# GLA mixer: states and outputs of two chunks at a time, their float32 products in one row

## The chip, the core and the metric

One Trainium2 chip, one of its cores. The core has five engines that run their own instruction lists and wait for each other by semaphores: PE (matmuls into PSUM), DVE and ACT (elementwise work, both can read PSUM), POOL (elementwise work outside PSUM) and SP (here it only issues DMAs). In a profile, PEld is PE's weight load, which overlaps its matmuls. The metric is device microseconds of one execution, the median of the runs.

## What is computed

Two layers on x of shape (1, 1024, 1024): a gated linear attention (GLA) layer with four heads, then a Mamba-2 layer. The change lies in the GLA layer. Of its reference, per head, with q, k, a of 128 columns and v of 512:

```python
def step(S, inp):
    qi, ki, vi, ai = inp
    b = jnp.cumsum(ai, axis=-2)
    o_inter = jnp.einsum('bhcd,bhdv->bhcv', qi * jnp.exp(b), S)
    ...
    o = o_inter + jnp.einsum('bhij,bhjv->bhiv', attn, vi)
    b_last = b[:, :, -1:, :]
    S = jnp.exp(b_last[:, :, 0, :, None]) * S + jnp.einsum(
        'bhjd,bhjv->bhdv', ki * jnp.exp(b_last - b), vi)
    return S, o
...
o = rmsnorm(o, w_head_norm).reshape(bsz, L, GLA_DV) * jax.nn.silu(g.astype(jnp.float32))
return o.astype(h.dtype) @ w_out
```

## The kernel before

The sequence is cut into two halves of 512 tokens (t = 0 and 1) and each half into four chunks of 128 tokens (the result does not depend on the chunk's size). The program is GLA on half 0, GLA on half 1, then the Mamba-2 layer on both. Large projections are "units" of 12 matmuls with 512 columns each: both operands are split into a float32r high and low part, and three products are summed (`mm3`, L223 to L225; L469 to L471 for v). Their PSUM tiles are called pp, the weight tiles wh and wl: ACT casts the high part (L171), POOL subtracts to get the low part (L176), four units ahead of PE.

The mixer of a head is a generator (`mixer`) that advances beside the units: after each unit, some of its steps are emitted, and a scheduler then sets the order on each engine, PE's too, from what it thinks is ready. The mixer's PSUM tiles are called mb; there are four of them in turn. For the part that changes:

- `split(c)` makes the high and low part of v of chunk c (ACT L649, POOL L650).
- `state(c, parts)` is three float32r matmuls of 512 columns into one mb tile: the chunk's addition to the state S (PE L223 to L225 with mb<-t,ktok). A step of DVE then makes the next S (L717 for the first, L719), in one of four tiles x.
- The outputs of a chunk are, for each of four blocks of 128 columns, a float32 matmul of S with qd (L712, left out where there is no S yet) and one of v with at (L713), into an mb tile po. The trace shows a float32 matmul as two records.
- po is then copied to SBUF: two blocks by ACT (L726), two by DVE (L727), into o0 and o1 (o2 in the code).
- After four chunks: squares and their sum on ACT and POOL, silu gate times output on POOL (L737), the norm's sum over partitions on PE (L292, L293), a chain on DVE and ACT (L299, L311 to L313, L745) and the high and low parts yh and yl (ACT L748, DVE L749), which the units of the output projection take (pp<-yh,wh).

In the last half, no state is made after the last chunk (nst is 3).

Of the kernel before, what the change touches and what calls it, by code (L numbers as in the profile page):

```python
# [14 lines left out]
ALU = mybir.AluOpType  # L15

P = 128
T = 512
# [3 lines left out]
NC = T // P  # L22
# [3 lines left out]
ORDER = mybir.DependencyInfo(mybir.DependencyClass.NoSync, mybir.DependencyReason.DATA)  # L26
# [27 lines left out]
def hybrid_kernel(ctx: ExitStack, tc: tile.TileContext, xT, w_in0, w_gk, w_up, w_out0,  # L54
                  w_in1, w_dt, w_out1, par, masks, tri, out):
    nc = tc.nc
    V, A, G, PE = nc.vector, nc.scalar, nc.gpsimd, nc.tensor
    dma = nc.sync.dma_start
# [12 lines left out]
    def tl(tag, bufs, shape=(P, T), dt=F32):  # L71
        cnt[0] += 1
        return sb.tile(list(shape), dt, name=f"{tag}_{cnt[0]}", tag=tag, bufs=bufs)

    def ps(tag):
        cnt[0] += 1
        return (psp if tag == "pp" else psm).tile([P, T], F32, name=f"{tag}_{cnt[0]}", tag=tag)

    def tmp(n=P):
        t = tl("t", NTMP)  # L80
        return t[:] if n == P else t[0:n, :]

    def c3(ap, w=P):
        return ap.rearrange("p (n w) -> p n w", w=w)
# [5 lines left out]
    def act(out, in_, func, **k):  # L90
        name = SILU if func == AF.Silu else LN_EXP
        i = None
        if name != table[0]:
            i = A.preload_act_table_set(name)
            for m in table[2]:
                tc.add_manual_dep(i.ins, m.ins.name, ORDER, reason="table")
            table[:] = name, i, []
        o = A.activation(out, in_, func, **k)
        tc.add_manual_dep(o.ins, table[1].ins.name, ORDER, reason="table")
        table[2].append(o)  # L100
        return o


    pr = cst.tile([P, N_PAR], F32, name="pr")
# [17 lines left out]
    at = cst.tile([P, NC, P], F32, name="at")  # L122

    def late_constants():
        mskf = tmp()
        dma(mskf[:, 0:N_MASK], masks)
        dma(trim[:], tri)
        G.memset(a64[:], 0.0)
        G.memset(at[:], 0.0)
        V.tensor_copy(msk[:], mskf[:, 0:N_MASK])  # L130
        V.tensor_tensor(idd[:], ident[0:64, 0:32], ident[0:64, 32:64], op=ALU.add)
        act(ea_log[:], pr[0:32, C_AL:C_AL + 1], AF.Exp)
# [5 lines left out]
    S_carry = [dram.tile([P, T], F32, name=f"S_{h}") for h in range(GH)]  # L138
# [83 lines left out]
    def mm3(o, lh, ll, rh, rl, first, last):  # L222
        PE.matmul(o, lh, rh, start=first, stop=False)  # L223
        PE.matmul(o, lh, rl, start=False, stop=False)  # L224
        PE.matmul(o, ll, rh, start=False, stop=last)  # L225
# [71 lines left out]
    def rstd_of(p, n, box, var, stay=False):  # L297
        v = tmp() if var is None else var
        V.tensor_scalar(v, p[:], 1.0 / n, EPS, op0=ALU.mult, op1=ALU.add)  # L299
        r = p[:] if stay else tl("rstd", 3)[:]  # L300
        l = tmp()
        act(l, v, AF.Ln)
        act(l, l, AF.Exp, scale=-0.5)
        newton(V, r, v, l)
        box.append(r)
        yield
# [102 lines left out]
    class Gla:  # L409
# [115 lines left out]
        def mixer(self, h):  # L525
# [7 lines left out]
            V.tensor_tensor(wup[64:96, :], wraw[64:96, :], wup[64:96, :].bitcast(F32), op=ALU.subtract)  # L533
            S = None
            if t:
                S = tl("x", 4)[:]
                dma(S, S_carry[h][:])
            yield
# [4 lines left out]
            m, l = tmp(), tmp()  # L543
# [5 lines left out]
            for c in range(NC):  # L549
                cs = slice(c * P, (c + 1) * P)  # L550
# [9 lines left out]
            dec = tl("decg", 2, (P, NC))  # L560
# [6 lines left out]
            qd = tl("x", 4)[:]  # L567
# [61 lines left out]
            for c in range(NC):  # L629
                cs = slice(c * P, (c + 1) * P)  # L630
                PE.transpose(ptk[:, cs], kd[:, cs], ident[:])

            o2 = [tl(tag, 1, (P, 2, T))[:] for tag in ("o0", "o1")]
# [9 lines left out]
            v = self.v[h]  # L643
            nst = NC - 1 if t == NT - 1 else NC

            def split(c):
                if c < nst:
                    vh, vl = tl("t", NTMP, dt=F32R)[:], tl("t", NTMP, dt=F32R)[:]
                    A.copy(vh, v[c])  # L649
                    G.tensor_tensor(vl, v[c], vh.bitcast(F32), op=ALU.subtract)  # L650
                    return vh, vl
# [5 lines left out]
            last = []  # L657

            def half_columns(o, lhsT, rhs):
                m = PE.matmul(o, lhsT, rhs, start=True, stop=True)  # L660
                if last:
                    tc.add_manual_dep(m.ins, last[-1].ins.name, ORDER, reason="columns")
                last.append(m)

            def products(p, kk, qq, w, c0, c1):
                for c in range(c0, c1):
                    for hh in range(2):
                        ks, qs, o = c * P + hh * 64, (2 * (c - c0) + hh) * w, (c - c0) * w
                        half_columns(p[hh * 64:hh * 64 + 64, o:o + w], kk[:, ks:ks + 64], qq[:, qs:qs + w])
                return p[:, 0:(c1 - c0) * w]  # L670
# [5 lines left out]
            for c in range(NC):  # L676
                half_columns(p64[c], d[:, c * P:c * P + 64], d[:, c * P + 64:(c + 1) * P])
# [11 lines left out]
            vp = split(0)  # L689
# [3 lines left out]
            o = [o2[vb // 2][:, vb % 2, :] for vb in range(4)]  # L693
            def state(c, parts):
                if c < nst:
                    p = ps("mb")
                    cs = slice(c * P, (c + 1) * P)
                    mm3(p[:], kh[:, cs], kl[:, cs], *parts, True, True)
                    return p

            pst = state(0, vp)
            vp = split(1)
            for g in self.g[h]:
                act(g, g, AF.Silu)
            yield
            for c in range(NC):
                cs = slice(c * P, (c + 1) * P)
                po = ps("mb")
                for vb in range(4):
                    vs = slice(vb * P, (vb + 1) * P)  # L710
                    if S is not None:
                        PE.matmul(po[:, vs], S[:, vs], qd[:, cs], start=True, stop=False)  # L712
                    PE.matmul(po[:, vs], v[c][:, vs], at[:, c, :], start=(S is None), stop=True)  # L713
                if c < nst:
                    Sn = tl("x", 4)[:]
                    if S is None:
                        V.tensor_copy(Sn, pst[:])  # L717
                    else:
                        V.scalar_tensor_tensor(Sn, S, dec[:, c:c + 1], pst[:], op0=ALU.mult, op1=ALU.add)  # L719
                    S = Sn  # L720
                    if c == NC - 1:
                        dma(S_carry[h][:], S)
                pst = state(c + 1, vp)
                vp = split(c + 2)
                yield
                A.copy(o2[0][:, :, cs], c3(po[:, 0:256]))  # L726
                V.tensor_copy(o2[1][:, :, cs], c3(po[:, 256:T]))  # L727
            yield


# [12 lines left out]
            for vb in range(4):  # L743
# [3 lines left out]
                c = tl("yl", 6, dt=F32R)[:]  # L747
# [486 lines left out]
    def mixq(g, h, rate):  # L1234
        return [[Lazy(lambda: g.mixer(h)), rate, 0.0]]
# [6 lines left out]
    for p in range(2):  # L1242
        g = ph[p]
        for h in range(GH):
            o = [lambda: g.outp(h - 1)] if h else ([lambda: ph[0].outp(3)] if p else [])
# [16 lines left out]
    for p in range(2, 4):  # L1262
        s = ph[p]
        for g in range(SG):
# [18 lines left out]
            elif p == 3 and g == SG - 2:  # L1283
# [3 lines left out]
                last = mixq(s, g + 1, 1.0)[0]  # L1287
# [120 lines left out]
```

## Time and profile before

| | |
|---|---|
| median of 3 runs | 1597.12 us (1595.63 to 1600.03) |
| profiled execution, its own time | 1597.23 us |
| its span from first to last instruction | 1595.5 us |
| mean granted TensorE clock | 0.997 of full speed |
| busy share PE / PEld | 98% / 82% |
| busy share DVE / ACT / POOL | 58% / 60% / 41% |

A busy share is averaged over the whole span. PE's is made of matmuls whose ends are modelled, so what a matmul costs is better read from start to start. The GLA mixers lie between about 56 and 760 us.

### The profile page before, as it was taken

What the parts mean: (1) busy time and instruction counts of PE and PEld (TensorE: products, weight loads), DVE (VectorE), ACT (ScalarE), POOL (GpSimd) and SP (SyncE); (2) the same over time, 40 slices, a digit from 0 to 9 for tenths busy, and PEclk for the clock granted to TensorE, in tenths of its full rate; (3) what the DMA queues carried; (4) which work ended last, traced back from release to release, by engine and by line L of the source; (5) the groups of instructions that cost most, each with busy time, mean ns of one, the idle gap of its engine ahead of it and who ended that gap; (6) DMA issues with size and microseconds to landing.
All of it is one profiled execution on the core that took longest, in us unless ns stands there. A gap on an engine that the chain in (4) does not pass through costs nothing.

```text
span 1595.5 us, 24009 instructions
## 1 busy us (share of the span) xinstructions
PE 1566.5 (98%) x8272; PEld 1304.9 (82%) x8272; DVE 919.1 (58%) x1579; ACT 955.2 (60%) x1804; POOL 651.2 (41%) x542
## 2 busy tenths in 40 slices
PE   7999999999999999999999999999999999999996
PEld 5787888888888888888888888888878888888886
DVE  7355557595516245396735445447967963355657
ACT  4455455564627355474866757666667677767843
POOL 6455565643320111227345665666513222222322
PEclk9999999999999999999999999999999999999999
DMA  7544566565675465554685565666765776655752
GB/s 237 190 152 145 167 193 198 174 208 161 206 249 178 155 202 185 172 187 141 198 283 163 185 210 189 187 201 198 246 197 197 242 230 217 201 182 187 264 190 86
DMA packets 172746, 309.30 MB, mean 194 GB/s; under 512 B 19088, under 2 KB 25104, under 8 KB 172624
## 3 DMA queue, kind: packets, MB, share of 16 engines
q1 hardware_dynamic: 172624, 307.77, 60.3%
q8 instruction: 65, 1.06, 0.3%
q14 instruction: 57, 0.47, 0.1%
HBM read 232.06 MB, written 75.63 MB: 193 GB/s over the span
## 4 chain that ended last, share of the span: by engine, by line
PE 84%; DVE 5%; ACT 5%; DMA 4%; issue 1%; POOL 1%; SPq 0%; DVEq 0%; POOLq 0%; ACTq 0%
PE pp L223 20%; PE pp L224 20%; PE pp L225 20%; PE pp L469 4%; PE pp L471 4%; PE pp L470 4%; PE mb L713 2%; PE mb L712 2%; PE mb L959 2%; PE mb L660 2%; DMA wraw<-w_in 1%; PE mb L952 1%; DMA v<-a_cum 1%; PE mb L223 1%; PE mb L224 1%
## 5 line engine op out<-in xcount | busy, mean ns | idle before, releaser
L171 ACT CAST wh<-wraw 128x512 fp32r<-128x512 f32 x472 | 289.8, 618 | 354.1 <-PE pp L224 136.9
L223 PE MATMUL pp<-hh,wh 128*128 128x512 f32 x1184 | 467.9, 396 | 8.7 <-ACT wh L171 7.6
L224 PE MATMUL pp<-hl,wh 128*128 128x512 f32 x1184 | 464.1, 392 | 1.2 <-DVE hl L371 1.2
L225 PE MATMUL pp<-hh,wl 128*128 128x512 f32 x1184 | 462.8, 391 | 0.0
L176 POOL TENSOR_TENSOR wl<-wraw,wh 128x512 fp32r<-128x512 f32 x240 | 322.5, 1352 | 313.2 <-ACT wh L171 245.0
L223 PEld LDWEIGHTS pp<-hh,wh 128*128 128x128 f32 x1184 | 222.7, 188 | 59.5 <-ACT wh L171 9.0
L224 PEld LDWEIGHTS pp<-hl,wh 128*128 128x128 f32 x1184 | 223.0, 188 | 48.6 <-DVE hl L371 3.1
L225 PEld LDWEIGHTS pp<-hh,wl 128*128 128x128 f32 x1184 | 222.9, 188 | 46.1
L223 PE MATMUL pp<-yh,wh 128*128 128x512 f32 x448 | 177.0, 397 | 2.6 <-DVE acc L515 1.2
L225 PE MATMUL pp<-yh,wl 128*128 128x512 f32 x448 | 176.0, 393 | 0.0
L224 PE MATMUL pp<-yl,wh 128*128 128x512 f32 x448 | 175.6, 392 | 0.0
L469 PE MATMUL pp<-wh,hh 128*128 128x512 f32 x256 | 99.9, 393 | 2.7 <-DVE m L444 2.7
L223 PEld LDWEIGHTS pp<-yh,wh 128*128 128x128 f32 x448 | 84.2, 188 | 22.3 <-ACT acc L889 2.4
L650 POOL TENSOR_TENSOR t<-v,t 128x512 fp32r<-128x512 f32 x28 | 39.3, 1414 | 153.4 <-ACT t L649 98.2
L470 PE MATMUL pp<-wl,hh 128*128 128x512 f32 x256 | 100.4, 392 | 0.0
L471 PE MATMUL pp<-wh,hl 128*128 128x512 f32 x256 | 100.0, 393 | 0.0
L225 PEld LDWEIGHTS pp<-yh,wl 128*128 128x128 f32 x448 | 84.1, 188 | 18.8
L224 PEld LDWEIGHTS pp<-yl,wh 128*128 128x128 f32 x448 | 84.2, 188 | 18.2 <-DVE yl L749 0.3
L830 DVE SCALAR_TENSOR_TENSOR m<-pp,pr,m 128x509 f32<-128x509 f32 (+2 forms) x96 | 70.5, 744 | 43.4 <-ACT m L827 42.4
L321 POOL TENSOR_TENSOR ss<-ss,t 128x512 f32<-128x512 f32 x53 | 75.1, 1417 | 42.5 <-ACT t L320 32.3
L830 DVE SCALAR_TENSOR_TENSOR x<-pp,pr,x 128x509 f32<-128x509 f32 (+2 forms) x96 | 71.2, 744 | 32.1 <-ACT x L827 30.9
L1041 POOL TENSOR_TENSOR t<-t,o 128x512 fp32r<-128x512 f32 x32 | 42.2, 1322 | 94.0 <-ACT o L1039 93.9
(287 smaller groups left out, 2593.9 us busy)
## 6 DMA issues: line engine op xcount, KB each, us to landing
wraw<-w_in SPq DMA_DIRECT2D x352, 256.0 KB, 3.6
low_in<-wl SPq DMA_DIRECT2D x176, 256.0 KB, 3.9
wl<-low_in SPq DMA_DIRECT2D x176, 256.0 KB, 3.1
wraw<-w_out SPq DMA_DIRECT2D x128, 256.0 KB, 3.4
low_out<-wl SPq DMA_DIRECT2D x64, 256.0 KB, 3.8
v<-a_cum SPq DMA_DIRECT2D x64, 256.0 KB, 3.8
wl<-low_out SPq DMA_DIRECT2D x56, 256.0 KB, 3.1
xn<-x SPq DMA_DIRECT2D x43, 256.0 KB, 3.7
```

Of the source, the lines that this page charges most:

```text
L171: A.copy(hi[:, 0:w], raws[n][:, 0:w])
L176: G.tensor_tensor(lo[:, 0:w], raws[n][:, 0:w], hi[:, 0:w].bitcast(F32), op=ALU.subtract)
L223: PE.matmul(o, lh, rh, start=first, stop=False)
L224: PE.matmul(o, lh, rl, start=False, stop=False)
L225: PE.matmul(o, ll, rh, start=False, stop=last)
L321: eng.tensor_tensor(ss, ss, sq, op=ALU.add)
L469: PE.matmul(o, rh[kb][:, cs], wh[:], start=(kb == 0), stop=False)
L470: PE.matmul(o, rh[kb][:, cs], wl[:], start=False, stop=False)
L471: PE.matmul(o, rl[kb][:, cs], wh[:], start=False, stop=(kb == KB - 1))
L650: G.tensor_tensor(vl, v[c], vh.bitcast(F32), op=ALU.subtract)
L830: V.scalar_tensor_tensor(dst[:, s:], o[:, 0:T - s], col(C_CW + j * 32 + si), dst[:, s:], op0=ALU.mult, op1=ALU.add)
L1041: G.tensor_tensor(xel[-1], xe, hi.bitcast(F32), op=ALU.subtract)
```

## The change

The four passes of a loop over chunks become two pairs. The states of chunks 0 and 1 come first, then the outputs of both chunks, chunk 1 ahead of chunk 0; then the states of 2 and 3, then their outputs. Within a pair, each float32 matmul is made to follow the one before it in PE's order (`behind`, which only orders; other matmuls may still be put between). The pair's two PSUM tiles are taken at once and copied out together. No instruction is added and none removed; the number of yields in this part, six, stays.

```diff
+    def behind(m, last):
+        if last:
+            tc.add_manual_dep(m.ins, last[-1].ins.name, ORDER, reason="columns")
+        last.append(m)
...
+            def outputs(c, Ss):
+                last, po = [], [ps("mb") for _ in range(2)]
+                for i in (1, 0):
+                    cs = slice((c + i) * P, (c + i + 1) * P)
+                    for vb in range(4):
+                        vs = slice(vb * P, (vb + 1) * P)
+                        if Ss[i] is not None:
+                            behind(PE.matmul(po[i][:, vs], Ss[i][:, vs], qd[:, cs], start=True, stop=False), last)
+                        behind(PE.matmul(po[i][:, vs], v[c + i][:, vs], at[:, c + i, :], start=(Ss[i] is None),
+                                         stop=True), last)
+                return po
...
-            for c in range(NC):
-                cs = slice(c * P, (c + 1) * P)
-                po = ps("mb")
-                for vb in range(4):
-                    vs = slice(vb * P, (vb + 1) * P)
-                    if S is not None:
-                        PE.matmul(po[:, vs], S[:, vs], qd[:, cs], start=True, stop=False)
-                    PE.matmul(po[:, vs], v[c][:, vs], at[:, c, :], start=(S is None), stop=True)
-                if c < nst:
-                    Sn = tl("x", 4)[:]
...
-                pst = state(c + 1, vp)
-                vp = split(c + 2)
-                yield
-                A.copy(o2[0][:, :, cs], c3(po[:, 0:256]))
-                V.tensor_copy(o2[1][:, :, cs], c3(po[:, 256:T]))
-            yield
+            S1 = step(S, 0, pst)
+            pst = state(1, vp)
+            vp = split(2)
+            yield
+            po = outputs(0, (S, S1))
+            S = step(S1, 1, pst)
+            pst, vp = state(2, vp), split(3)
+            yield
+            evac(0, po)
+            S3 = step(S, 2, pst)
+            pst = state(3, vp)
+            yield
+            po = outputs(2, (S, S3))
+            S = step(S3, 3, pst)
+            if S is not None:
+                dma(S_carry[h][:], S)
+            yield
+            evac(2, po)
+            yield
```

`evac(c, po)` is the two copies (now L731 and L732) for both chunks of the pair, and `step` the DVE instruction that makes the next S (now L710 and L712). Lines of the changed kernel lie 6 higher in `mm3` and before the mixer, up to 29 higher behind it.

The order that the scheduler makes of it differs at these places. PE, first head of half 0, from the last projection matmul ahead of the first outputs (mb_190 holds the outputs of chunk 0, mb_192 the state of chunk 1, mb_203 the outputs of chunk 1); before:

```order
L469 MATMUL pp_199_988<-wh_216_1077,hh5_34_197 128x512
L713 MATMUL mb_190_964<-at_86,v_113_566 128x128 x4
L223 MATMUL mb_192_971<-t_188_955,ktok_157_758 128x512
L224 MATMUL mb_192_971<-t_189_956,ktok_157_758 128x512
L225 MATMUL mb_192_971<-t_188_955,t_158_759 128x512
L712 MATMUL mb_203_1007<-x_146_708,x_191_969 128x128
L713 MATMUL mb_203_1007<-at_86,v_114_568 128x128
```

The same place in the changed kernel (mb_203 holds the outputs of chunk 1, mb_202 those of chunk 0, mb_205 and mb_212 the states of chunks 2 and 3):

```order
L476 MATMUL pp_198_983<-wl_209_1025,hh4_27_180 128x512
L723 MATMUL mb_203_1001<-x_146_708,x_190_964 128x128
L477 MATMUL pp_198_983<-wh_208_1024,hl4_28_181 128x512
...
L476 MATMUL pp_200_985<-wl_209_1025,hh4_27_180 128x512
L724 MATMUL mb_203_1001<-at_86,v_114_568 128x128
...
L724 MATMUL mb_202_1000<-at_86,v_113_566 128x128 x4
L229 MATMUL mb_205_1016<-t_192_970,ktok_157_758 128x512
...
L229 MATMUL mb_212_1050<-t_206_1020,ktok_157_758 128x512
```

The state of chunk 1 has moved ahead of all outputs. The first float32 matmul stands alone, six projection matmuls ahead of the rest of its pair; then the other eleven follow each other, and then two states in a row.

DVE, the same head, from the second S on (x is S; o1 is the copy of a po); before:

```order
L727 COPY o1_150_723<-mb_190_964 128x2x128
L719 SCALAR_TENSOR_TENSOR x_204_1016<-x_191_969,decg_141_682,mb_192_971 128x512
L727 COPY o1_150_723<-mb_203_1007 128x2x128
L719 SCALAR_TENSOR_TENSOR x_212_1057<-x_204_1016,decg_141_682,mb_205_1018 128x512
L727 COPY o1_150_723<-mb_211_1048 128x2x128
```

and in the changed kernel:

```order
L712 SCALAR_TENSOR_TENSOR x_204_1014<-x_190_964,decg_141_682,mb_191_966 128x512
L732 COPY o1_150_723<-mb_203_1001 128x2x128
L732 COPY o1_150_723<-mb_202_1000 128x2x128
L712 SCALAR_TENSOR_TENSOR x_211_1048<-x_204_1014,decg_141_682,mb_205_1016 128x512
L712 SCALAR_TENSOR_TENSOR x_215_1072<-x_211_1048,decg_141_682,mb_212_1050 128x512
L732 COPY o1_150_723<-mb_214_1055 128x2x128
L732 COPY o1_150_723<-mb_213_1054 128x2x128
```

The third S (x_211), which the second pair of outputs needs, now stands behind the two copies of the first pair.

ACT, third head of half 0, behind the table load that follows the gates' silu (t is the high part of a chunk of v, v_433 that of chunk 1); before:

```order
L94 ACT_TABLE_LOAD
L171 CAST wh_528_2594<-wraw_512_2484 128x512
L320 ACTIVATE t_534_2625<-xn_508_2473 128x512
L171 CAST wh_535_2628<-wraw_520_2538 128x512
L649 CAST t_540_2654<-v_433_2151 128x512
L171 CAST wh_542_2663<-wraw_526_2573 128x512
```

and in the changed kernel:

```order
L94 ACT_TABLE_LOAD
L177 CAST wh_535_2628<-wraw_520_2538 128x512
L177 CAST wh_542_2663<-wraw_526_2573 128x512
L326 ACTIVATE t_534_2625<-xn_508_2473 128x512
L177 CAST wh_551_2698<-wraw_530_2600 128x512
L655 CAST t_540_2654<-v_433_2151 128x512
```

The split of chunk 1 now stands behind the cast of a weight three units further on (wh_551, wh_552 before).

## Rows read from the trace of the kernel before

**Rows 1.** The page, part 1: busy us, share of the span, instructions.

```profile
PE 1566.5 (98%) x8272; PEld 1304.9 (82%) x8272; DVE 919.1 (58%) x1579; ACT 955.2 (60%) x1804; POOL 651.2 (41%) x542
```

**Rows 2.** Busy time by stage: stretch, length, then busy of each engine.

```profile
core 0: us, PE busy (x) PEld busy (x) DVE busy (x) ACT busy (x) POOL busy (x), PEclk, DMA share, GB/s
60.00:400.00 340.00, 338.46 (x1779) 281.88 (x1778) 207.11 (x403) 183.10 (x328) 182.30 (x142) 1.00 0.56 175
400.00:760.00 360.00, 360.00 (x1892) 300.81 (x1891) 188.59 (x386) 188.77 (x346) 93.39 (x74) 1.00 0.58 186
```

**Rows 3.** PE's waits between 60 and 760 us, all there are.

```profile
PE pp L223 <- DVE acc L515: 1.2, 1, 1.2
PE pp L223 <- ACT yh L748: 0.3, 1, 0.3
```

**Rows 4.** Timeline of PE, first head of half 0: start, length, instruction.

```profile
99.82 0.39 PE L469 MATMUL pp<-wh,hh 128*128 128x512 f32 x1
...
105.94 0.39 PE L469 MATMUL pp<-wh,hh 128*128 128x512 f32 x1
106.17 1.05 PE L713 MATMUL mb<-at,v 128*128 128x128 f32 x8
...
107.53 0.39 PE L225 MATMUL mb<-t,t 128*128 128x512 f32 x1
107.77 0.38 PE L712 MATMUL mb<-x,x 128*128 128x128 f32 x2
...
109.32 0.39 PE L713 MATMUL mb<-at,v 128*128 128x128 f32 x2
109.47 0.48 PE L223 MATMUL mb<-t,ktok 128*128 128x512 f32 x1
...
110.25 0.40 PE L470 MATMUL pp<-wl,hh 128*128 128x512 f32 x1
```

**Rows 5.** Timeline of PE at the end of that head's mixer.

```profile
136.14 0.39 PE L293 MATMUL mb<-t,onr 128*128 128x512 f32 x1
...
143.86 0.39 PE L225 MATMUL pp<-hh,wl 128*128 128x512 f32 x1
144.58 0.47 PE L223 MATMUL pp<-yh,wh 128*128 128x512 f32 x1 [0.34 <-ACT yh L748]
145.09 0.50 PE L224 MATMUL pp<-yl,wh 128*128 128x512 f32 x1
```

**Rows 6.** Timelines of ACT, POOL and DVE at that end.

```profile
117.00 0.37 ACT L726 COPY o<-mb 128x256 f32<-128x256 f32 x1 [2.12 <-PE mb L713]
...
117.45 5.09 POOL L737 TENSOR_TENSOR sg<-o,sg 128x512 f32<-128x512 f32 x4 [3.17 <-ACT o L726]
...
131.76 1.36 DVE L290 TENSOR_TENSOR t<-ss,t 128x512 fp32r<-128x512 f32 x1 [13.93 <-ACT t L289]
136.57 0.69 DVE L299 TENSOR_SCALAR t<-mb 128x512 f32<-128x512 f32 x1 [3.44 <-PE mb L293]
...
144.35 0.68 DVE L749 TENSOR_TENSOR yl<-mb,yh 128x512 fp32r<-128x512 f32 x1
```

**Rows 7.** Timelines of ACT and DVE: copies of a po and a step of S.

```profile
107.26 0.37 ACT L726 COPY o<-mb 128x256 f32<-128x256 f32 x1 [1.13 <-PE mb L713]
...
107.67 0.42 DVE L727 COPY o<-mb 128x256 f32<-128x256 f32 x1 [6.76 <-ACT o L726]
108.01 0.74 DVE L719 SCALAR_TENSOR_TENSOR x<-x,decg,mb 128x512 f32<-128x512 f32 x1
```

**Rows 8.** Timelines, same head: last copy of at, two weights' low parts, PE's use.

```profile
101.69 0.40 ACT L688 COPY at<-a 64x256 f32<-64x256 f32 x1
...
123.74 2.53 POOL L176 TENSOR_TENSOR wl<-wraw,wh 128x512 fp32r<-128x512 f32 x2
...
130.44 0.39 PE L225 MATMUL pp<-hh,wl 128*128 128x512 f32 x1
```

**Rows 9.** Timelines, third head of half 0: PE's first state, a weight's cast on ACT.

```profile
259.51 0.39 PE L223 MATMUL mb<-t,ktok 128*128 128x512 f32 x1
...
260.34 0.62 ACT L171 CAST wh<-wraw 128x512 fp32r<-128x512 f32 x1 [0.51 <-DMA wraw<-w_in]
```

More of the change, by code (lines that the diff above doesn't have):

```diff
@@ L659, in half_columns @@
             def half_columns(o, lhsT, rhs):
[L660 to L663, printed above, removed]
+                behind(PE.matmul(o, lhsT, rhs, start=True, stop=True), last)
             def products(p, kk, qq, w, c0, c1):
@@ L699, in state, with step, evac @@
                     return p
+            def step(S, c, p):
+                if c >= nst:
+                    return None
+                Sn = tl("x", 4)[:]
+                if S is None:
+                    V.tensor_copy(Sn, p[:])
+                else:
+                    V.scalar_tensor_tensor(Sn, S, dec[:, c:c + 1], p[:], op0=ALU.mult, op1=ALU.add)
+                return Sn
+            def outputs(c, Ss):
[9 more added lines that the diff above has]
+                return po
+            def evac(c, po):
+                for i in range(2):
+                    cs = slice((c + i) * P, (c + i + 1) * P)
+                    A.copy(o2[0][:, :, cs], c3(po[i][:, 0:256]))
+                    V.tensor_copy(o2[1][:, :, cs], c3(po[i][:, 256:T]))
             pst = state(0, vp)
@@ L705, in mixer @@
             yield
-            for c in range(NC):
-                cs = slice(c * P, (c + 1) * P)
-                po = ps("mb")
-                for vb in range(4):
-                    vs = slice(vb * P, (vb + 1) * P)
-                    if S is not None:
-                        PE.matmul(po[:, vs], S[:, vs], qd[:, cs], start=True, stop=False)
-                    PE.matmul(po[:, vs], v[c][:, vs], at[:, c, :], start=(S is None), stop=True)
-                if c < nst:
-                    Sn = tl("x", 4)[:]
[L716 to L722, printed above, removed]
-                pst = state(c + 1, vp)
-                vp = split(c + 2)
-                yield
-                A.copy(o2[0][:, :, cs], c3(po[:, 0:256]))
-                V.tensor_copy(o2[1][:, :, cs], c3(po[:, 256:T]))
+            S1 = step(S, 0, pst)
[16 more added lines that the diff above has]
+            evac(2, po)
             yield
```

## The prediction

> **What bounds the kernel now.** I first ask which engine is full. The page's first part shows PE busy for 98% of the span and the others for 60% at most [rows 1]. A share is an average, so I look at the two stages in which the GLA mixers run: between 60 and 400 us (half 0) PE is busy 338.46 of 340.00 us, between 400 and 760 us (half 1) all of 360.00 [rows 2]. PE's waits in the two stages are only two, 1.2 and 0.3 us [rows 3]. So the mixers lie under a PE that never stops, and a change to them can move the time in two ways alone: by what PE's own matmuls cost, or by a new wait of PE. To be sure that PE is full and not merely marked busy, I read start to start: from 99.82 to 105.94 us lie 27 steps of float32r matmuls with 512 columns [rows 4], 0.2267 us each, with no slack in between.
>
> There is a rule against this reading. The Trainium skill (Perfetto Trace Analysis, Identifying the Most-Contended Engine) says that matmul busy time is no good measure of headroom, and that the busy share of the weight loads is one. That share is 82% here, and by it PE would have 18% of room and swallow small waits. The steps of 0.2267 us say that a wait comes on top, and I go by them.
>
> **The change, part by part.**
>
> *Fewer switches between float32r and float32.* Each row of output matmuls is a float32 run inside float32r ones. Its price is read at the run that begins at 107.77 us. From the float32r start at 107.53 to the one at 110.25 are 2.72 us [rows 4]. In them lie four float32r steps, 0.907 us, and eight float32 matmuls. The rows from 107.77 to 109.32 are seven of these in 1.55 us, 0.2214 each, so eight are 1.771. The rest, 0.04 us, is what the run costs for going in and out. In the orders of the two programs I count the runs of output matmuls: 33 before, 19 after (sixteen would be the two per head; the first three heads have one stray matmul ahead of the first pair). Fourteen fewer at 0.04 us are **-0.6 us**. Bounds: nothing, if a longer run costs as much more; if all 33 could go, 1.3 us. The matmuls themselves are the same in number and shape, hence nothing.
>
> *Where the pair has to wait for its inputs.* The first pair needs the copies of at; in head 0 of half 0 the last of them ends at 102.09, and the first matmul that reads at starts at 106.17 us [rows 8, 4]. In the changed order as many float32r matmuls, give or take one, stand ahead of that point, so 4 us of cover are left: 0. The second pair needs the third S and the PSUM tiles of the first. That is a copy by ACT, 0.37 us, two by DVE, 0.42 each, and a step, 0.74 [rows 7]: 1.95 us from the end of the first pair. The order puts at least 26 float32r matmuls there in every head, 5.9 us. Cost 0, and without that cover 1.95 us for each of eight heads.
>
> *The end of a mixer.* In half 1 the last output matmul stays where it was in the stream, and in the other heads of half 0 the output projection comes long after the norm. Head 0 of half 0 is the tight one. PE issues the norm's L293 at 136.14 us; DVE waits for it (3.44 us, L299 at 136.57), and from there a chain of DVE and ACT runs to yl, which begins at 144.35 [rows 5, 6]. PE starts the last projection matmul at 143.86, would go on at 144.09, starts the first output projection matmul at 144.58 and the second at 145.09 instead of 0.23 later: 0.49 + 0.28 = 0.77 us late. In the changed order 128 projection matmuls instead of 125 stand between the first state and L293, and 31 instead of 34 behind it up to the output projection. So L293 and the chain start 3 x 0.2267 = 0.68 us later, while PE arrives when it did: **+0.7 us**. Does L293 get its input by then? The last output matmul has 47 instead of 41 projection matmuls ahead of it, 1.36 us; ACT copies at 117.00, POOL's silu products start at 117.45, and the low part of the sum is ready at 131.76 + 1.36 = 133.12 us [rows 6], so 134.5 after, against 136.8. POOL begins its four products 1.4 us later too, and behind them stand weights: the first is ready at about 125.0 and used at 130.44 us [rows 8], so 5.4 us of cover become 4.0. What is late next is DVE's sum at L515, for which PE waits 1.2 us now [rows 3]; DVE and PE are both 0.7 later there, so that wait stays. Bounds for the whole part: -2 us, if the two waits vanish by better placing, and +1.4 us, if the chain takes the whole delay.
>
> *ACT's queue in the third head.* There the split of chunk 1 is now queued behind the cast of a later weight, and the state of chunk 1 stands only four projection matmuls behind that of chunk 0, where it had some forty. Before, the first state started at 259.51 us, and that cast at 260.34, waiting for the weight's DMA [rows 9]. The stream places this head's first state 12 matmuls later (2.7 us), the next one a state and four matmuls after it (1.6), and its low part is read one step later: 259.51 + 4.5 = 264.0 us. If the cast still ran at 260.34, ACT would be through with it and the split at 261.6, and POOL with a weight and the split (1.27 each, from the pair of 2.53 us) [rows 8] at 264.1: a wait of 0.1 us. Since the order also moves an earlier weight's cast ahead of the silus, the buffer should come free sooner: **0**, with 3 us as the upper bound if the DMA lands that much later.
>
> *Behind the GLA layer* the orders are the same, row by row, on all five engines, so nothing moves there.
>
> The sum is made on the profiled execution, 1597.23 us, which is 0.1 above the median of 1597.12: 1597.23 - 0.6 + 0.7 = **1597.3 us**. A measurement of this kernel tells about 0.3%, 4.8 us, from no change.
>
> **The rivals.**
>
> *The change does not do what it says.* Going in and out of float32 costs nothing that a longer run does not cost again. Then only the head's end counts: 1597.9. It speaks for this that the price, 0.04 us, is little more than the rounding of the rows. The verdict would be the same.
>
> *The switch is dearer than I read, and the time falls.* To gain 4.8 us, each of the fourteen would have to cost 0.38 us, 0.34 more than I read. Rows 4 speak against it: the whole excess has to fit between the starts shown. Time 1592; chance 0.03.
>
> *PSUM tiles become the wait, and the time rises.* Two of the four mb tiles are now held until both chunks are done. If the second pair came before the first is copied out, PE would stand still for up to 1.95 us in each of eight heads, 15.6 us together, 1612. It decides from fewer than nine float32r matmuls between the pairs (1.95 / 0.2267); there are 26 or more, unless DVE or ACT are more than 3.9 us behind with other work. In the dense third and fourth head of half 0 that could be, so at two heads rather than eight: some 2 us each, 1601. The Trainium skill (Perfetto Trace Analysis, Optimization Strategy) warns of consistent bubbles where buffers are too few for the next tile; no wait for an mb tile is among rows 3. Chance of a rise over 0.3%: 0.05.
>
> *The split comes too late.* If the casts ahead of it wait for a DMA as in the third head, PE waits up to 3 us there, and if heads 0 and 1 suffer too, up to 9: 1600 to 1606. Against it: in heads 0 and 1 nothing has moved ahead of the split of chunk 1. Chance 0.07, most of it at one head, which is still within 0.3%; over it 0.03.
>
> **How the numbers follow.** The forecast, with the first rival, has 0.85, the dear switch 0.03, the PSUM wait 0.05 and the late split 0.07. The range takes in -2 - 0.6 below (1594.6) and one head's 3 us and the 0.7 above (1601), and a little at the lower end for the scatter of the runs (1595.63 lowest): 1594.2 to 1601.2. Slower by over 0.3% is 0.05 + 0.03 and 0.01 for what I did not see, 0.09; faster 0.03 and 0.01, 0.04; the rest, 0.87, is within it.
>
> **What would show it.** In the changed kernel's profile, PE's waits between 60 and 760 us should again be two, near 144.5 us (for yh or yl, about 0.7 us longer) and near 158 us (DVE's sum). The timeline of the first head should show twelve float32 matmuls in a row at 0.22 us each, with about 0.04 us more around the run. A PE wait in front of an output matmul, for DVE or ACT, would be the PSUM rival; one in front of the second matmul of a state, for POOL, the late split. I am wrong if such waits add up to more than 4.8 us, or if steps outside these places change.

## The result

The changed kernel takes 1599.82 us (median of 19 runs, 1597.75 to 1602.41), the kernel before 1595.96 (19 runs, 1592.27 to 1600.03). The ratio is 1.0025, with an interval of 1.0018 to 1.0032: about 4 us slower, within 0.3%, but clear of no change. The forecast was 1597.3, with a range of 1594.2 to 1601.2; it expected +0.1 us. Twelve later runs (e9 below) gave 1.0022 (1.0011 to 1.0032).

The page of the changed kernel, part 1, answers to [rows 1] (busy us, share of the span, instructions). The numbers are almost the same, so they don't show where 4 us went:

```profile
PE 1567.1 (98%) x8272; PEld 1304.3 (82%) x8272; DVE 928.7 (58%) x1579; ACT 956.1 (60%) x1804; POOL 648.5 (41%) x542
```

PE's waits between 60 and 760 us are three now, and answer to [rows 3]. L229, L521 and L425 were L223, L515 and L419:

```profile
PE mb L229 <- DVE a L631: 1.8, 1, 1.8
PE pp L229 <- DVE sg L425: 1.3, 1, 1.3
PE pp L229 <- DVE acc L521: 1.0, 1, 1.0
```

Waits alone don't add up to the difference, since a matmul can also take longer without a wait. So I compare the time between two marks at which the order of PE is the same in all kernels: the start of the 193rd and of the 2801st matmul into a pp tile. In between lie all GLA mixers. The rows of the two marks on PE's timeline, kernel before and then the changed one:

```profile
61.63 0.39 PE L225 MATMUL pp<-hh,wl 128*128 128x512 f32 x1
...
765.59 0.51 PE L224 MATMUL pp<-hl,wh 128*128 128x512 f32 x1
```

```profile
59.73 0.39 PE L231 MATMUL pp<-hh,wl 128*128 128x512 f32 x1
...
767.88 0.51 PE L230 MATMUL pp<-hl,wh 128*128 128x512 f32 x1
```

That is 703.96 us before and 708.15 after, +4.19: the whole difference lies there, as the forecast assumed. With marks in between (the 769th, 1201st and 1585th such matmul; 221.86, 334.87 and 437.63 us in the kernel before) it splits into +1.44 for the first head, +1.78 up to the end of the third, +1.07 for the fourth, and -0.10 for all of half 1. Each part can be found in the timeline.

**First head, +1.4.** PE comes to the output projection and waits. The row answers to that of 144.58 us in [rows 5]:

```profile
144.12 0.47 PE L229 MATMUL pp<-yh,wh 128*128 128x512 f32 x1 [1.32 <-DVE sg L425]
```

The wait was 0.34 us and is 1.32, +0.98. The matmul needs a pp tile, and the last to read that tile is DVE's L425 (sg<-pp), which takes the output of a gate's projection and stands behind the norm's chain in DVE's queue. DVE's rows, kernel before (L419) and then the changed one:

```profile
143.75 0.68 DVE L419 TENSOR_TENSOR sg<-pp,rstd 128x512 f32<-128x512 f32 x1
```

```profile
143.29 0.68 DVE L425 TENSOR_TENSOR sg<-pp,rstd 128x512 f32<-128x512 f32 x1
```

They end at 144.43 and 143.97, and PE starts 0.15 us later in both. So the tile is what PE waited for before the change, too: the row in [rows 5] names ACT's yh, but the first of those casts began at 142.56 us. The chain starts 0.68 us later against PE, as forecast, and takes 0.30 longer. ACT now has a weight's cast between the chain's logarithm and its exponential (both L98):

```profile
136.53 0.63 ACT L98 ACTIVATE t<-t 128x512 f32<-128x512 f32 x1 [0.90 <-DVE t L305]
137.22 0.62 ACT L177 CAST wh<-wraw 128x512 fp32r<-128x512 f32 x1
137.75 0.63 ACT L98 ACTIVATE t<-t 128x512 f32<-128x512 f32 x1
```

That costs 0.55 us (2.60 from DVE's L305 to its L317, where 2.05 were), and 0.25 come back behind it, since the one DVE operation of the chain that is written long there took 1.41 us and not 1.67.

Another 0.4 us are lost 24 us earlier, when the next projection needs a pp tile that ACT frees late (L484, behind the squares and a cast): PE's step from 119.74 to 120.25 is 0.51 and the next 0.34, where 0.23 each is usual.

```profile
119.74 0.39 PE L477 MATMUL pp<-wh,hl 128*128 128x512 f32 x1
120.25 0.50 PE L229 MATMUL pp<-hh,wh 128*128 128x512 f32 x1
120.59 0.39 PE L230 MATMUL pp<-hl,wh 128*128 128x512 f32 x1
```

**Third head, +1.8.** PE's timeline: the products of the scores (L666), and then the first state:

```profile
258.66 1.31 PE L666 MATMUL mb<-raw,m 128*64 128x160 f32 x16
...
263.55 0.47 PE L229 MATMUL mb<-t,ktok 128*128 128x512 f32 x1 [1.80 <-DVE a L631]
```

The state needs an mb tile, and all four hold products. DVE frees one with its masked copies (L627, L631). DVE's timeline shows what stands ahead of these: two sums for the statistics of the other half (L327) and four accumulations (L521), 4.8 us from 257.30 to 262.11. The two sums are written as 1.41 and 1.16 us, though the one at 255.99 took 0.70; POOL had nothing to do then, and ran without a break from 258.07 us. Whether that is the reason was not tried.

```profile
257.30 1.32 DVE L521 TENSOR_TENSOR acc<-pp,acc 128x512 f32<-128x512 f32 x2
258.50 1.41 DVE L327 TENSOR_TENSOR ss<-ss,t 128x512 f32<-128x512 f32 x1
...
260.43 1.16 DVE L327 TENSOR_TENSOR ss<-ss,t 128x512 f32<-128x512 f32 x1
...
262.11 1.09 DVE L627 COPY_PREDICATED a<-msk,mb 128x96 f32<-128x96 uint8 x4
263.10 0.30 DVE L631 COPY_PREDICATED a<-msk,mb 128x128 f32<-128x128 uint8 x1
```

In the kernel before, the copies began 1.6 us after the products (257.53 and 255.92 us), and not 3.45; two matmuls of the output projection stood between products and state, and nobody waited. Its rows of PE and of DVE; the state starts at 259.51 [rows 9]:

```profile
255.92 1.31 PE L660 MATMUL mb<-raw,m 128*64 128x160 f32 x16
...
257.53 1.10 DVE L621 COPY_PREDICATED a<-msk,mb 128x96 f32<-128x96 uint8 x4
258.52 0.30 DVE L625 COPY_PREDICATED a<-msk,mb 128x128 f32<-128x128 uint8 x1
```

**Fourth head, +1.1.** Eight narrow matmuls (32 output columns each, the low-rank gate of the next half, L268 before, L274 now) stood in one row. In the kernel before, PE's timeline has them as one group of 16 records:

```profile
372.65 0.39 PE L225 MATMUL pp<-hh,wl 128*128 128x512 f32 x1
372.97 1.92 PE L268 MATMUL pp<-t,w 128*32 128x512 f32 x16
374.82 0.50 PE L469 MATMUL pp<-wh,hh 128*128 128x512 f32 x1
375.16 0.40 PE L470 MATMUL pp<-wl,hh 128*128 128x512 f32 x1
```

In the changed kernel the row of outputs, L723 and L724, stands in the middle of them:

```profile
370.32 0.39 PE L231 MATMUL pp<-hh,wl 128*128 128x512 f32 x1
370.63 1.06 PE L274 MATMUL pp<-t,w 128*32 128x512 f32 x6
...
371.96 0.39 PE L476 MATMUL pp<-wl,hh 128*128 128x512 f32 x1
...
376.00 0.39 PE L724 MATMUL mb<-at,v 128*128 128x128 f32 x2
376.32 1.90 PE L274 MATMUL pp<-t,w 128*32 128x512 f32 x10
378.15 0.50 PE L476 MATMUL pp<-wl,hh 128*128 128x512 f32 x1
378.49 0.39 PE L477 MATMUL pp<-wh,hl 128*128 128x512 f32 x1
```

From the matmul ahead of a group to the second one behind it, less the usual steps (0.23 us for each of two float32r matmuls, or 0.22 and 0.23 where a float32 one leads), it took 2.05 us in one group, and 1.19 + 2.04 = 3.2 in two. The single records say why: up to four of them start within 0.03 us of each other, and the next ones 0.41 to 0.44 us later. Each narrow matmul is two records, and those for the same 32 columns start one behind the other. So sixteen records in a row are four passes of four. Cut in two, six are two passes of three, and ten are four passes, the last two with one record each (377.20 and 377.63 us). Two more passes are some 0.85 us, and the rest is the second way in and out.

### The profile page after: what moved, and what is told of

Read it like the earlier page. It is cut to its first block, busy times and chain, and to the rows that moved or that the text cites. A ratio compares the mean times of both kernels' runs of the same rounds, so it can differ in the third digit from the quotient of the medians.

```text
span 1598.8 us, 24007 instructions
## 1 busy us (share of the span) xinstructions
PE 1567.1 (98%) x8272; PEld 1304.3 (82%) x8272; DVE 928.7 (58%) x1579; ACT 956.1 (60%) x1804; POOL 648.5 (41%) x542
## 4 chain that ended last, share of the span: by engine, by line
PE 83%; DVE 7%; ACT 4%; DMA 3%; issue 1%; POOL 1%; SPq 0%; DVEq 0%; POOLq 0%; ACTq 0%
PE pp L229 20%; PE pp L230 19%; PE pp L231 19%; PE pp L476 4%; PE pp L475 4%; PE pp L477 4%; PE mb L988 2%; PE mb L724 2%; PE mb L723 2%; PE mb L981 1%; PE mb L666 1%; DMA wraw<-w_in 1%; PE mb L229 1%; PE mb L230 1%; PE mb L231 1%
## 5 line engine op out<-in xcount | busy, mean ns | idle before, releaser
L229 PE MATMUL pp<-hh,wh 128*128 128x512 f32 x1184 | 467.5, 396 | 8.9 <-ACT wh L177 7.5
L182 POOL TENSOR_TENSOR wl<-wraw,wh 128x512 fp32r<-128x512 f32 x240 | 320.4, 1342 | 315.5 <-ACT wh L177 247.1
L229 PEld LDWEIGHTS pp<-hh,wh 128*128 128x128 f32 x1184 | 223.0, 188 | 60.5 <-ACT wh L177 9.1
L229 PE MATMUL pp<-yh,wh 128*128 128x512 f32 x448 | 176.9, 397 | 2.8 <-DVE sg L425 1.3
L229 PEld LDWEIGHTS pp<-yh,wh 128*128 128x128 f32 x448 | 84.2, 188 | 21.9 <-ACT wh L177 1.7
L327 POOL TENSOR_TENSOR ss<-ss,t 128x512 f32<-128x512 f32 x53 | 75.8, 1431 | 44.1 <-ACT t L326 33.5
```

The costliest lines, as they stand in the source:

```text
L182: G.tensor_tensor(lo[:, 0:w], raws[n][:, 0:w], hi[:, 0:w].bitcast(F32), op=ALU.subtract)
L327: eng.tensor_tensor(ss, ss, sq, op=ALU.add)
```

## The experiments

Theory A: the pairs as such cost nothing; the scheduler set the work in other places, and three of these are bad. Theory B: the pairs cost, by longer float32 rows or by the two mb tiles that they hold. The table has the time between the marks, as difference to the kernel before in us, and behind it the Mamba-2 layer (from the 2801st to the 5821st pp matmul), whose order is the same in all of these (e3 stands below, since its order there differs):

```
run                        head 1  heads 2, 3  head 4  half 1  sum    Mamba-2 layer
before                     0       0           0       0       703.96 814.05
changed                    +1.44   +1.78       +1.07   -0.10   708.15 814.88
e9 changed, again          +1.45   +1.79       +1.07   -0.10   708.17 817.25
e1 gate group together     +1.44   +1.79       -0.12   -0.10   706.97 813.45
e2 statistics later        +1.41   +0.49       +1.88   -0.10   707.63 815.15
e4 state later             +1.41   +0.80       +1.07   -0.10   707.13 816.73
e5 chunk 0 first           -1.04   -0.01       -0.03   -0.10   702.78 815.78
e6 (same program as e5)    -1.71   -0.01       +0.61   -0.10   702.75 820.23
e7 squares on DVE          -1.61   +0.03       +0.14   -0.10   702.42 819.47
e8 before, squares on DVE  -2.37   +0.05       +0.02   0       701.66 812.57
e10 both                   -1.82   +0.23       +0.13   -0.10   702.41 811.58
```

**e9_changed_again.** No edit; it tells how far such numbers can be trusted.

> The changed kernel as it is, once more. In the mixers' stage (between the marks, 708.15 us in its first profile) every theory expects the same waits to 0.02 us, 1.32, 1.80 and the group in two, since the order is fixed: 708.1 to 708.3. The Mamba-2 layer behind, whose order is the same in all kernels and which took 812.6 to 820.2 us in single profiles of runs one to eight, may come out anywhere in that range. The median: 1.0025 of the kernel before, or 1.000 if the first difference was the Mamba-2 layer's scatter; by the mixers' stage alone it should be 1.0026.

708.17 us beside 708.15, with the waits of 1.81 and 1.31 us again, and the median 1.0022 of the kernel before. PE's order in the first head is the same in six of the profiles (the changed kernel, e9, and e1 to e4), and that head is 1.41 to 1.45 us longer in all six. What scatters lies mostly outside the marks: the first comes at 59.7 to 61.6 us, though the order ahead of it is the same everywhere. So a profile tells more of this stage than a median of ten runs, which can't tell 1 us. But it isn't fixed to 0.02 us where a DMA comes last: e6 below turns out to be e5 run a second time, and single heads differ there by up to 0.67 us, at a sum that differs by 0.03.

**e1_gate_together.** The narrow matmuls are ordered behind the last outputs ahead of them:

```diff
-                    PE.matmul(o[32 * j:32 * (j + 1), :], w[:, 4 * hf + j, :], rows[j], start=(hf == 0), stop=(hf == 1))
+                    m = PE.matmul(o[32 * j:32 * (j + 1), :], w[:, 4 * hf + j, :], rows[j], start=(hf == 0), stop=(hf == 1))
+                    behind(m, last_o)
...
+                last_o[:] = last[-1:]
                 return po
```

> The changed kernel, with the eight narrow gate matmuls of the next half (32 columns of output each) ordered behind the last outputs of the fourth head, so that they stand together again; PE's order is otherwise the same up to there. Theory A (the change costs by the places into which the order falls): the matmuls L274, which in the changed kernel stand in two groups of 6 and 10 records with 3.3 us for both, take 2.1 us in one group again, and nothing else moves: 1599.8 - 1.3 = 1598.5 us. Theory B (the pairs themselves cost: longer float32 rows, PSUM tiles held longer): the time stays at 1599.8, and the 1.3 us come back at another place of that head. One run can't tell 1.3 us; the trace of the place can.

```profile
375.95 1.93 PE L276 MATMUL pp<-t,w 128*32 128x512 f32 x16
377.80 0.50 PE L478 MATMUL pp<-wh,hh 128*128 128x512 f32 x1
```

PE's timeline has one group of 16 records again, and the fourth head goes from +1.07 to -0.12: 1.19 us come back, and nothing else moves. The single time of 1599.71 us says nothing on 1 us. Theory B fails for this head.

**e2_stats_later** and **e4_state_later** ask what the third head's state waits for. e2 takes DVE's sums away:

```diff
-                        mix.append([stats(p + 1), 0.5, 0.0])
+                        mix.append([stats(p + 1), 0.5, -8.0 if p == 0 else 0.0])
```

> The changed kernel, with the norm statistics of the other half (DVE's sums ss) begun 16 units later in the third head of half 0, so that DVE has three operations instead of six between its last product of the gates and the first copy of the scores. Theory A1: PE's wait of 1.8 us ahead of that head's first state is for DVE, which has to free the state's PSUM tile and does this behind sums and accumulations; it falls from 1.8 to under 0.3 us. Theory A2, that of the prediction's rival: the wait is for the low part of v that POOL makes, or for the cast on ACT behind a DMA; then it stays above 1 us. Theory B (the pairs): it stays too. The order of the fourth head shifts with it, so its gate group may fall elsewhere.

DVE's timeline now has it idle until the products are there, and PE starts the state without a wait:

```profile
257.66 0.69 DVE L521 TENSOR_TENSOR acc<-pp,acc 128x512 f32<-128x512 f32 x1 [1.97 <-PE pp L231]
259.05 1.12 DVE L627 COPY_PREDICATED a<-msk,mb 128x96 f32<-128x96 uint8 x4 [0.70 <-PE mb L666]
```

```profile
260.70 0.63 PE L666 MATMUL mb<-t 128*64 128x64 f32 x8
261.26 0.50 PE L229 MATMUL mb<-t,ktok 128*128 128x512 f32 x1
```

The wait of 1.8 us is gone, as A1 has it; POOL and the low part (A2) had no share in it. But the work went somewhere: at 306.11 us a projection waits 0.23 us for ACT (0.5 with the slow step behind it), and in the fourth head a state waits 0.65 for the same copies. Of the 1.3 us that the third head won, 0.8 were given back in the fourth. The single runs of e2 and e4 took 1601.76 and 1601.96 us, which can't tell such amounts. e4 leaves DVE alone and moves the state:

```diff
+            if h == 2 and t == 0:
+                yield
+                yield
             pst = state(0, vp)
```

> The changed kernel, with two more steps of the mixer of the third head ahead of its first state, which puts twelve projection matmuls (2.7 us) between the products of the scores and that state, where none stood. DVE's queue keeps its sums and gets one more ahead of the copies of the scores. Theory A1: the wait ahead of the first state is gone (1.8 + 0.7 - 2.7, below nothing). Theory B: a wait of the same size appears at the pair of outputs of that head. Where the fourth head's gate group falls is open; if it is still split, its 1.3 us stay.

```profile
260.70 2.87 DVE L327 TENSOR_TENSOR ss<-ss,t 128x512 f32<-128x512 f32 x2
...
264.10 1.11 DVE L627 COPY_PREDICATED a<-msk,mb 128x96 f32<-128x96 uint8 x4
```

```profile
265.54 0.47 PE L229 MATMUL mb<-t,ktok 128*128 128x512 f32 x1 [0.59 <-DVE a L631]
```

A miss in size: the wait fell to 0.59 us and not to nothing, since DVE's copies came some 1.7 us later than in the changed kernel, where I had counted 0.7 for one more sum; the two sums in a row are written with 2.87 us. It is the same wait for the same line. At the pair of outputs nobody waits, against B.

**e3_more_switches.** The outputs of half 1 are spread over the projection's matmuls (the list todo holds them two by two):

```diff
+    def alone(m):
+        if todo:
+            last = [m]
+            for f in todo.pop(0):
+                behind(f(), last)
+            todo_after.append(last[-1])
...
+            m = PE.matmul(o, l, r, start=st, stop=sp)
+            if todo_after:
+                behind(m, [todo_after.pop()])
+            alone(m)
```

> The changed kernel, with the output matmuls of half 1 spread: after each of eight float32r matmuls stand two float32 ones, instead of sixteen in a row. The eight float32 runs of half 1 become 64. The prediction priced a switch in and out at 0.04 us: 56 more give +2.2 us between 400 and 760 us. Read from half 1 of the two traces (17 runs before, 8 after, 0.10 us less over the same work) it is 0.011: +0.6 us. A dear switch of 0.38 would give +21 us. Nothing else in half 1 should wait.

From 453.44 us on, PE's timeline has two float32 matmuls, one float32r, and again two, as meant. Between the 1585th and the 2501st pp matmul lie the outputs of three heads: 12 float32 runs before, 6 in the changed kernel, 48 here. The stretch is 246.41 us before, 0.05 less in the changed kernel, 0.05 more here. So 6 runs fewer save 0.05 us (0.008 each) and 42 more cost 0.10 (0.002 each). A switch costs next to nothing, less even than my second figure. The run as a whole took 1608.03 us, which none of the theories gave. Its profile is 7.4 us longer than that of the changed kernel (1606.2 and 1598.8 us): 1.7 of it lie ahead of the first mark and 6.7 in the Mamba-2 layer (821.57 us), less 1.1 for outputs that here come behind the mark. The order at the layer's beginning falls otherwise in this kernel; PE's waits between 770 and 910 us sum to 0.9 in the changed kernel (all for L862), and here the longest are 2.0 us for ACT's L1090 (two waits), 1.2 for its L98 and 0.6 for POOL's L182.

**e5_chunk0_first** turns the order within a pair round, and **e6_states_only** was meant to keep the paired states alone:

```diff
-                for i in (1, 0):
+                for i in (0, 1):
```

> The changed kernel with one thing turned round: within a pair the outputs of the earlier chunk come first. In the order that follows, no float32 matmul stands alone ahead of its pair, the gate group of the fourth head stands together, the third head's first state has two projection matmuls between it and the products again, and 43 projection matmuls (34 before the change, 31 in the changed kernel) stand between the first head's norm and its output projection. Theory A (the places): the +1.4, +1.8 and +1.1 us of heads one, three and four are gone, and the 0.8 us that the kernel before waits at the end of the first head too; half 1 keeps its -0.1: 1596.0 - 0.9 = 1595.1 us. Theory B (rows of two chunks, two PSUM tiles held): as the changed kernel, 1599.8 us.

> The changed kernel with only half of the change: states two at a time, but the outputs of each chunk copied out as soon as they are there, not as a pair, and chunk 0 ahead of chunk 1. PE's matmuls stand as in the run with chunk 0 first. Theory A: no wait at the three places, the stage of the mixers as long as in that run to 0.3 us. Theory B: shorter than in that run, by what holding two tiles costs, up to 2 us for each of the heads.

In e5, PE's timeline has the first pair begin with chunk 0 (8 records of L724, with L723 right behind), two matmuls of the projection ahead of the third head's state, and the narrow matmuls together:

```profile
106.01 1.05 PE L724 MATMUL mb<-at,v 128*128 128x128 f32 x8
...
257.14 0.63 PE L666 MATMUL mb<-t 128*64 128x64 f32 x8
257.70 0.51 PE L230 MATMUL pp<-yl,wh 128*128 128x512 f32 x1
258.04 0.40 PE L231 MATMUL pp<-yh,wl 128*128 128x512 f32 x1
258.28 0.39 PE L229 MATMUL mb<-t,ktok 128*128 128x512 f32 x1
...
371.66 1.92 PE L274 MATMUL pp<-t,w 128*32 128x512 f32 x16
```

With the pairs kept, the stage is 702.78 us, 5.4 less than in the changed kernel and 1.2 less than before. The time is 1595.79 (11 runs), ratio 0.9997 (0.9987 to 1.0008), where the stage alone gives 0.9993. One expectation missed: a wait of 0.73 us is left at the end of the first head, for DVE's L425. ACT's timeline has the reason: the cast between the chain's logarithm and exponential had to wait for its own DMA.

```profile
135.51 0.63 ACT L98 ACTIVATE t<-t 128x512 f32<-128x512 f32 x1 [1.51 <-DVE t L305]
136.91 0.62 ACT L177 CAST wh<-wraw 128x512 fp32r<-128x512 f32 x1 [0.77 <-DMA wraw<-w_out]
137.43 0.63 ACT L98 ACTIVATE t<-t 128x512 f32<-128x512 f32 x1
```

What went is the later wait, for DVE's accumulation (1.2 us in [rows 3]).

e6 does not test what it was made for. The scheduler makes the same program of it as of e5: though its source takes one tile at a time and copies it at once, the two traces have the same records in the same order on PE, DVE, ACT and POOL. So e6 is a second profile of e5, and Theory B has no run in which tiles are held for a shorter time. As such it tells how far the stage repeats: 702.75 beside 702.78 us, but 0.67 less in the first head, where the cast waits for no DMA this time and PE for nothing, and 0.64 more in the fourth, where PE comes earlier and waits 0.38 us for ACT's L488. Its time of 1602.13 is one run, in which the Mamba-2 layer took 820.23.

On the held tiles there remain the traces, and in the changed kernel a pair does not hold its tiles to the end. ACT's rows in the first head, of the second pair:

```profile
114.72 0.37 ACT L731 COPY o<-mb 128x256 f32<-128x256 f32 x1 [2.93 <-PE mb L724]
116.51 0.37 ACT L731 COPY o<-mb 128x256 f32<-128x256 f32 x1 [1.41 <-PE mb L724]
```

The pair's last record starts on PE at 116.19 us: the first tile is copied while the row goes on.

**e7_squares_on_dve** and **e8_before_squares_on_dve** give the first head's end more room, in the changed kernel and in the one before:

```diff
-                square_into(ss, o[vb], vb == 0, G)
+                square_into(ss, o[vb], vb == 0, V if h == t == 0 else G)
```

> The changed kernel, pairs as they are (chunk 1 first), with one line edited: in the first head of half 0, DVE instead of POOL sums the squares for the norm. DVE has nothing to do there for 14 us. The norm comes 32 projection matmuls (7.3 us) earlier, and the order behind it falls otherwise: the third head's first state gets two projection matmuls ahead of it, the gate group stands together. Theory A: the waits of 1.3, 1.8 us and the split group go, though the rows of pairs stay: 704.0 - 0.8 - 0.1 us between the marks, 1595.1 us in all, with 0.4 more if the wait for a projection's PSUM tile near 120 us stays. Theory B: the rows cost wherever they stand, at least 1598.

> The kernel before with the same line edited: DVE sums the squares of the first head. Its own waits at the end of that head, 0.49 and 0.28 us, should go: 1596.0 - 0.8 = 1595.2 us, which 5 rounds may just tell from no change. If the last sum of DVE (1.2 us of PE's waiting at 158 us) is moved away too, 1594.

In both, no wait of PE between 60 and 760 us is listed any more. e7 keeps the pairs and chunk 1 first, and its stage is 702.42: the three places of the changed kernel don't come from that order alone, and go once the work falls elsewhere. It took 1596.73 us, 0.9993 (0.9982 to 1.0004). e8 has the shortest stage of all and the lowest median, 1594.74 (11 runs), 0.9987 (0.9979 to 0.9996) of the kernel before, by 2.3 us between the marks: the 0.8 at the end of the first head, the 1.2 at 158 us, and 0.3 around them. In the runs its interval overlaps those of e5, e7 and e10. With the squares edited alike, the kernel with pairs is 0.76 us longer between the marks than the one without (e7 and e8); 0.47 of it is the step near 122 us of the next paragraph.

**e10_both** puts e5 and e7 together.

> Chunk 0 first and the squares of the first head on DVE together. Theory A: the end of the first head waits for nothing, the pairs are worth 0.1 us, so the mixers' stage is that of the kernel before with the squares on DVE, 701.7, less 0.1: 701.6 us, and the time 0.9985 of the kernel before. If pairs cost where heads follow each other closely, 702.4 or more, as in the run with chunk 1 first.

702.41 us, and not 701.6; 1597.26 us, 0.9997 (0.9984 to 1.0010). 702.4 is the figure that the expectation gave to a cost of the pairs, and it is 0.75 over e8. 0.5 of this is one place: near 122 us PE waits for ACT's L484, which frees a pp tile. In the changed kernel and in e7, L484 comes right behind the squares and a cast. In e10 it stands behind the cast of the norm's sum, which waits for DVE:

```profile
120.73 0.62 ACT L295 CAST t<-ss 128x512 fp32r<-128x512 f32 x1 [1.21 <-DVE ss L327]
121.26 2.42 ACT L484 ACTIVATE v<-pp,rtok 128x512 f32<-128x512 f32 x4
```

In e8 the first two of these (L478) stand ahead of that cast, and in e5, with pairs, they start at 119.79 and PE does not wait. So this part is a place again. The other 0.2 to 0.3 us was not followed; that the pairs cost this much is not ruled out.

## Why the prediction was right, and where not

**What bounds the kernel** held in full: a PE that never stops, in which each wait adds its whole length. What was found, 0.98, 0.4, 1.8 and the 1.2 of the split group, less 0.1, makes 4.3 us, and the marks give 4.2. The busy share of the weight loads stayed at 82% and swallowed none of them: for this kernel the trace decides against that rule of the Trainium skill (Perfetto Trace Analysis, Identifying the Most-Contended Engine) as the prediction applies it.

**Fewer switches, -0.6 us:** the mechanism was right and the price not. Half 1, in which nothing else moves, gives 0.008 us for each run, e3 0.002. Fourteen runs are -0.1. The 0.04 that I read in [rows 4] was taken from one run, as a rest of 0.04 in 2.72; there the steps of the state's matmuls next to the run are 0.235 instead of 0.2267, and I put that down to the switch.

**The pair's inputs, 0:** right. No output matmul is listed with a wait in any of the kernels, and a pair does not hold both tiles until it is done, as the rival had it (ACT's copy at 114.72).

**The end of a mixer, +0.7:** right in place, with 0.98 measured, and right in that the chain comes later while PE does not. What PE waits for was misread: not yh or yl, but the pp tile that DVE's L425 empties behind the chain. The 0.3 over are the longer chain: from DVE's L305 to the first L774 it is 5.50 us, where 5.20 were, mostly by ACT's cast. The 0.4 near 120 us I did not see; the sum lacks it.

**ACT's queue in the third head, 0:** this step failed. I followed the low part of v through ACT and POOL to the state's matmuls, and had the state's place right (12 matmuls later). But a matmul has an output too: its mb tile was still read by DVE. Before the change it came free only 0.7 us ahead of the state (copies done at 258.82, state at 259.51): the queue on DVE ahead of the copies was the term to work out.

**What I left out:** the order of the units themselves. I had counted the runs of output matmuls and not looked at what they cut in two. The eight narrow matmuls cost 1.2 us in that way. The Trainium skill (TensorEngine Tiling (Array Packing), Key Properties) says that different tiles of the array can execute in parallel, and that a change of the tiling mode drains TensorE; the trace agrees with the first, with 0.41 to 0.44 us for four narrow records or for one. For the second it has about 0.3 us for one more way in and out, which fits; that this is the drain is not shown.

**The rivals.** A wait for a PSUM tile did come, as the third one had it, but for a tile that no pair held, and the late split did not. The time stayed within the range because every piece was small: to the forecast's +0.1 came +0.3 (chain), +0.4, +1.8 and +1.2 that I had not seen, and 0.5 of saving that was not there, 4.3 in all. That is luck in part: the upper end was set for one late split of 3 us, and other things filled it. By the last of the prediction's own signs, steps that change outside its places, it was wrong: the third head's state, the narrow matmuls and the step near 120 us are such places, and three waits are listed where it named two.

**The cause** of the 4 us is the places into which the work fell; what the pairs cost apart from them is at most the 0.2 to 0.3 us that e10 leaves open. e1 takes one place away and wins 1.19 us there; e5 turns round one decision of the change, chunk 1 ahead of chunk 0, and all three places are gone; e7 leaves that decision and moves the squares, and they are gone as well. `behind` has no part: in the program without it the order is the same on all five engines, row by row (read from the program; no run). Why the scheduler sets the work as it does when chunk 1 comes first was not tried.

## What to carry to other kernels

Where one engine never stops and a scheduler sets the order, an edit that adds no work is worth what its places are worth: go through the whole order for what has moved next to what, for each matmul through its inputs, its output tile and that tile's last reader, and look for rows that are cut in two. A tight place is the cheapest gain: moving three sums to an idle engine gave 2.3 us between the marks, where fourteen switches gave 0.1. Take the time between two marks in the profile for differences below the scatter of the runs, and profile twice where a DMA may come last. Compare the programs before comparing their times: two edits can leave the same one.

## What the hardware showed beyond that

- Going from float32r to float32 and back cost 0.002 to 0.008 us.
- One narrow matmul of 32 columns, left alone, took as long as four side by side (0.41 to 0.44 us, at the end of the group cut in two).
- A matmul into a PSUM tile started 0.15 us after the end of the DVE operation that last read the tile (144.58 behind 144.43 us, 144.12 behind 143.97, 263.55 behind 263.40).
- The same order gave the same time to 0.03 us in the mixers' stage as a whole (two kernels, two profiles each), with up to 0.67 us between single heads, but 811.6 to 820.2 us in the Mamba-2 layer. In e7 a weight arrived late there: ACT's cast at 887.85 us waited 2.94 us for the DMA, where it was 1.24 in the kernel before (887.65), and two operations of ACT later PE waited 1.64 us for ACT's L1068.
